# Strided attention on one core: semaphores of the kernel's own, and Q blocks cast whole

## The chip, the core and the metric

The kernel runs on one core of a Trainium2 chip. A core has TensorE (matrix multiply into PSUM), VectorE, ScalarE and GpSimd (elementwise work; the profile calls them PE, DVE, ACT and POOL), SyncE (SP), which here issues all transfers, and 16 DMA rings that carry them. The metric is device time in microseconds, the median of several runs. The profile is of one execution.

## What is computed

Attention in which every query attends to the same 16 keys, those at positions 0, 64, 128 and so on:

```python
batch, heads, seq, dim = (8, 12, 1024, 64)          # stride 64
attend_positions = np.arange(0, seq, stride)        # 16 positions
scores = np.einsum('bhqd,bhkd->bhqk', q, k) * scale # scale = 1/sqrt(dim)
weights = np.exp(scores - np.max(scores, axis=-1, keepdims=True))
weights = weights / (np.sum(weights, axis=-1, keepdims=True) + 1e-10)
result[:, :, i, :] = np.einsum('bhqk,bhkd->bhqd', weights, v)[:, :, 0, :]
```

All of Q (25.2 MB, float32) is read, and a result of the same size is written. Of K and V only 16 rows a head are needed, 0.4 MB each.

## The kernel before

The 96 heads are worked in 24 blocks of 4 heads. A block of Q is 1 MB: a tile `qn` of 128 partitions by 2048 float32. There are 10 `qn` buffers and 8 output buffers `out_sb`, also 1 MB each; `qb`, `qt` and `rec` have 2 each, the weights `w` and the values `v` 3 each.

Setup (lines 88 to 153): SyncE issues K, Q block 0, V and Q blocks 1 to 9. Meanwhile GpSimd builds an identity and the permutation `perm_v` from it (eight small copies, line 118), VectorE and GpSimd clear `k_t`, and VectorE works out which quarter of a group a partition belongs to (lines 132 to 148: `slot_i`, `slot_f`, `s_sel`, `mask`). `key_rows` and `keys` (lines 156 to 175) cast K, transpose it and place it into `k_t`, a third of the heads at a time. `value_rows` (line 177) spreads V over the partitions by a matmul.

A block g goes through these steps:

- `cast(g)`, line 197: float32 to bfloat16. GpSimd takes the first 1024 columns (line 200), ScalarE the other 1024 (line 201).
- `transpose(g)`, line 205: VectorE transposes `qb` into `qt`.
- `scores(g)`, lines 207 to 227: four matmuls (line 212) into one PSUM tile, then two exps on ScalarE (line 223) into `w`.
- `values(g)`, line 189: GpSimd multiplies V with the mask into `v` (line 191). The last 4 columns of `v` give the sum of the weights.
- `outputs(g, c)` for c = 0, 1, 2, line 230: three, two and three matmuls (line 237) into one of two PSUM tiles `o_ps`, then VectorE's reciprocal of the sums (line 245). For c = 0 and 1 VectorE multiplies into `out_sb` (line 247). For c = 2 ScalarE copies (line 249) and GpSimd multiplies in place (line 250).
- `store(g)`, line 252: SyncE issues the output of 1 MB, and then the load of block g+10 (line 298).

The order is written by hand (`ahead`, line 274, and the loop at line 284): in turn g come transpose(g+2), scores(g+1), values(g+2), cast(g+3), then outputs(g, 0..2), store(g) and load(g+10). Every engine works its own instructions in this order. The third of K that is needed later is prepared in turns 1 to 3 and 5 to 7.

The framework puts in the waits: it counts each engine's work with one semaphore an engine, and the transfers with eight, used in turn. So a transfer waits until the eighth before it has landed, and a wait for one instruction can be met only with a later one of the same engine.

Of the kernel before, what the change touches and what calls it, by code (L numbers as in the profile page):

```python
# [11 lines left out]
FP32 = mybir.dt.float32  # L12
BF16 = mybir.dt.bfloat16
# [29 lines left out]

@with_exitstack  # L50
def kernel(
# [24 lines left out]
    const = ctx.enter_context(tc.tile_pool(name="const", bufs=1))  # L76
    qn_pool = ctx.enter_context(tc.tile_pool(name="qn", bufs=QBUFS))
    out_pool = ctx.enter_context(tc.tile_pool(name="outsb", bufs=OBUFS))
    qb_pool = ctx.enter_context(tc.tile_pool(name="qb", bufs=2))
    qt_pool = ctx.enter_context(tc.tile_pool(name="qt", bufs=2))  # L80
    rec_pool = ctx.enter_context(tc.tile_pool(name="rec", bufs=2))
    psum_sc = ctx.enter_context(tc.tile_pool(name="psc", bufs=2, space=bass.MemoryType.PSUM))
    psum_o = ctx.enter_context(tc.tile_pool(name="po", bufs=2, space=bass.MemoryType.PSUM))

    ctx.enter_context(tc.manual_schedule())


    k_raw = const.tile([P, NC, D], FP32, name="k_raw")
    v_raw = const.tile([P, NC, D], FP32, name="v_raw")
    kv_src = [[stride * D, P], [2 * HG * SD, NC], [1, D]]  # L90
    qn = {}

    def load(g):
        qn[g] = qn_pool.tile([P, 32 * D], FP32, name="qn", tag="qn")
        n = P if g < 2 else 32
        _copy(nc, qn[g], _ap_with(Q, [[HG * SD // n, n], [1, HG * SD // n]], g * HG * SD))

    nc.sync.dma_start(k_raw, _ap_with(K, kv_src))
    load(0)
    nc.sync.dma_start(v_raw, _ap_with(V, kv_src))  # L100
# [3 lines left out]

    identity = const.tile([P, P], BF16, name="identity")
    make_identity(nc, identity)
    id_v = identity.rearrange("p (c b a k) -> p c b a k", c=2, b=2, a=2)

    perm_v = const.tile([P, 2, 2, 2, 2, NK], BF16, name="perm_v")

    iota_p = const.tile([P, 1], I16, name="iota_p")
    nc.gpsimd.iota(iota_p, pattern=[[0, 1]], base=0, channel_multiplier=1)
    col4 = const.tile([P, 4], I16, name="col4")
    nc.gpsimd.iota(col4, pattern=[[1, 4]], base=0, channel_multiplier=0)
    for c in range(2):
        for a in range(2):
            for e in range(2):
                nc.gpsimd.tensor_copy(
                    out=perm_v[:, c, a, :, e], in_=id_v[:, c, :, a]
                )  # L120

    k_t = const.tile([P, NG, 2, KW], BF16, name="k_t")
    nc.vector.memset(k_t[:, 0:8], 0.0)  # L123
    w_bufs = []
    for i in range(3):
        w = const.tile([P, 8, P], BF16, name=f"w{i}")
        nc.vector.memset(w, 0.0)  # L127
        w_bufs.append(w)
    nc.gpsimd.memset(k_t[:, 8:NG], 0.0)  # L129
# [9 lines left out]
    nc.vector.tensor_scalar(  # L139
        out=s_sel, in0=col4, scalar1=slot_f, scalar2=None, op0=ALU.is_equal  # L140
    )
    v_bufs = []
    for i in range(3):
        v = const.tile([P, 4 * D + 4], BF16, name=f"v{i}")
        nc.vector.tensor_copy(out=v[:, 4 * D :], in_=s_sel)
        v_bufs.append(v)
    mask = const.tile([P, 4, D], BF16, name="mask")
    nc.vector.tensor_copy(out=mask, in_=s_sel.unsqueeze(2).to_broadcast([P, 4, D]))

    k_bf = const.tile([P, NC, D], BF16, name="k_bf")  # L150
    k_r = const.tile([P, NC, D], BF16, name="k_r")
    v_bf = const.tile([P, NC, D], BF16, name="v_bf")
    v_rep = const.tile([P, NC, 2, D], BF16, name="v_rep")


    def key_rows(m):
        part = slice(4 * m, 4 * m + 4)
        nc.scalar.copy(k_bf[:, part], k_raw[:, part])  # L158
        nc.vector.transpose(  # L159
            k_r[:, part].rearrange("p n d -> p (n d)").bitcast(I32),  # L160
            k_bf[:, part].rearrange("p n d -> p (n d)").bitcast(I32),
        )


    def keys(m, c):
        for s in range(4):
            src, dst, col = 32 * (2 * c + s % 2), 32 * (2 * (s % 2) + s // 2), NK + 32 * s
            op = nc.vector.tensor_copy if m == 0 and s >= 2 else nc.scalar.copy
            op(  # L169
                k_t[dst : dst + 32, 8 * m + c : 8 * m + 8 : 2, :, col : col + NK],  # L170
                k_r[src : src + 32, 4 * m : 4 * m + 4].rearrange(
                    "p n (a k f) -> p a n f k", a=2, f=2
                )[:, s // 2],
            )


    def value_rows(n):
        for c in range(2):
            vp = psum_sc.tile([P, NC // 2, D], FP32, name="vp", tag="sc")
            nc.tensor.matmul(  # L180
                vp, lhsT=perm_v[:, c].rearrange("p a b e k -> p (a b e k)"),
                rhs=v_bf[:, 6 * n : 6 * n + 6], start=True, stop=True,
            )
            nc.vector.tensor_copy(out=v_rep[:, 6 * n : 6 * n + 6, c], in_=vp)  # L184

    qb, qt, wt, vb, rec, out_sb = {}, {}, {}, {}, {}, {}


    def values(g):
        vb[g] = v_bufs[g % 3]  # L190
        nc.gpsimd.tensor_tensor(  # L191
            out=vb[g][:, 0 : 4 * D].rearrange("p (s d) -> p s d", s=4), in0=mask,
            in1=v_rep[:, g // 2, g % 2].unsqueeze(1).to_broadcast([P, 4, D]),
            op=ALU.mult,
        )

    def cast(g):
        qb[g] = qb_pool.tile([P, 32 * D], BF16, name="qb", tag="qb")
        half = 16 * D
        nc.gpsimd.tensor_copy(out=qb[g][:, 0:half], in_=qn[g][:, 0:half])  # L200
        nc.scalar.copy(qb[g][:, half:], qn[g][:, half:])  # L201

    def transpose(g):
        qt[g] = qt_pool.tile([P, 32 * D], BF16, name="qt", tag="qt")
        nc.vector.transpose(qt[g].bitcast(I32), qb[g].bitcast(I32))  # L205

    def scores(g):
        sc = psum_sc.tile([P, 512], FP32, name="sc", tag="sc")
        q = qt[g]
        for e in range(2):  # L210
            for f in range(2):
                nc.tensor.matmul(  # L212
                    sc, lhsT=k_t[:, g, f, NK * (1 - e) : NK * (1 - e) + P],
                    rhs=_ap_with(
                        q, [q.ap[0], [D, 8], [16 * D, 2], [2, 32]],
                        extra_offset=8 * D * e + f,
                    ),
                    start=e + f == 0, stop=e + f == 2,
                )
        w = wt[g] = w_bufs[g % 3]  # L220
        for a in range(2):
            wa = w[64 * a : 64 * a + 64]
            nc.scalar.activation(  # L223
                out=_ap_with(wa, [wa.ap[0], [P, 8], [1, 2], [2, 32]], extra_offset=64 * a),
                in_=sc[64 * a : 64 * a + 64].rearrange("p (t x q) -> p t x q", t=8, x=2),
                func=AF.Exp, bias=0.0, scale=scale,
            )


    def outputs(g, c):  # L230
        if c == 0:
            out_sb[g] = out_pool.tile([P, 4, 8, D], FP32, name="out_sb", tag="out_sb")
            rec[g] = rec_pool.tile([P, 8, 4], FP32, name="rec", tag="rec")
        i0, n = ((0, 3), (3, 2), (5, 3))[c]
        ps = psum_o.tile([P, 3, 512], FP32, name="o_ps", tag="o")
        for i in range(n):
            nc.tensor.matmul(  # L237
                ps[:, i, 0 : 4 * D + 4], lhsT=wt[g][:, i0 + i], rhs=vb[g],
                start=True, stop=True,
            )  # L240
        r = rec[g][:, i0 : i0 + n]
        o = ps[:, 0:n, 0 : 4 * D].rearrange("p i (s d) -> p i s d", s=4)
        to = out_sb[g][:, :, i0 : i0 + n].rearrange("p s i d -> p i s d")
        by = r.unsqueeze(3).to_broadcast([P, n, 4, D])
        nc.vector.reciprocal(r, ps[:, 0:n, 4 * D : 4 * D + 4])  # L245
        if c < 2:
            nc.vector.tensor_tensor(out=to, in0=o, in1=by, op=ALU.mult)  # L247
        else:
            nc.scalar.copy(to, o)  # L249
            nc.gpsimd.tensor_tensor(out=to, in0=to, in1=by, op=ALU.mult)  # L250

    def store(g):
        o = out_sb[g]
        _copy(
# [3 lines left out]
        )  # L258
# [8 lines left out]
    nc.vector.tensor_copy(out=v_bf, in_=v_raw)  # L267
# [16 lines left out]
    for g in range(NG):  # L284
# [13 lines left out]
        if g + QBUFS < NG:  # L298
            load(g + QBUFS)
# [33 lines left out]
```

## Time and profile before

| | |
|---|---|
| median of 3 runs | 129.51 us (129.45 to 129.59) |
| span of the profiled execution, first to last instruction | 127.7 us |
| VectorE busy | 88.5 us (69%), 167 instructions |
| ScalarE busy | 86.1 us (67%), 120 instructions |
| GpSimd busy | 80.1 us (63%), 89 instructions |
| TensorE matmul busy | 63.5 us (50%), 292 instructions |
| moved by the DMA rings | 51.20 MB, 401 GB/s over the span |
| one Q block, from issue to landing | 16.0 us (median) |
| one output, from issue to landing | 14.8 us (median) |

"Busy" is the share of the span in which an engine executes. The time of the runs is taken around the whole program, so it is larger than the span of the profiled execution. The rows for groups of instructions read: line, engine, operation, output <- input, shape, count, busy time in us, mean ns of one, and after the second bar the idle time just before them and what ended most of it. The row of 40 digits for DMA gives the mean busy share of the 16 rings in 40 equal slices of the span, in tenths.

### The profile page before, as it was taken

To read this page: it belongs to the slowest core of one execution; us is meant where nothing else is said; L and a number is where in the kernel's file an instruction comes from. 1 tells how busy PE (TensorE), PEld (TensorE's weight loads), DVE (VectorE), ACT (ScalarE), POOL (GpSimd) and SP (SyncE) were. 2 spreads that over 40 slices of the span, in tenths; PEclk is the share of its full clock that TensorE was granted. 3 is DMA by queue.
4 is the path that set the end of the run, shared out by engine and by line. 5 is a ranking of instruction groups with operands and counts; after the bars stand their busy time and mean duration, and the time that the engine had idled before them with its cause. 6 is when DMAs were issued, how large, how long until landed. Compare 5 with 4: busy or idle time off the path is not lost.

```text
span 127.7 us, 1234 instructions
## 1 busy us (share of the span) xinstructions
PE 63.5 (50%) x292; PEld 29.8 (23%) x292; DVE 88.5 (69%) x167; ACT 86.1 (67%) x120; POOL 80.1 (63%) x89
## 2 busy tenths in 40 slices
PE   0006559256756628653696646366777646410000
PEld 0002223123322313332243313133423313200000
DVE  6956691869698696859769799797987976720000
ACT  4161917886999968999958979979787885320000
POOL 8933709554875876577866997969689694450000
PEclk9999999996799986999559999999856999955555
DMA  2999989998997998989989999999999999999980
GB/s 66 379 320 467 472 349 482 380 452 354 467 482 326 498 413 369 495 362 421 493 357 431 470 380 444 434 403 462 428 393 449 398 428 418 428 426 421 431 352 36
DMA packets 7911, 51.20 MB, mean 401 GB/s; under 512 B 3872, under 2 KB 3872, under 8 KB 3872
## 3 DMA queue, kind: packets, MB, share of 16 engines
q1 hardware_dynamic: 7904, 51.12, 96.7%
q8 instruction: 2, 0.03, 0.1%
q14 instruction: 5, 0.04, 0.1%
HBM read 25.95 MB, written 25.17 MB: 400 GB/s over the span
## 4 chain that ended last, share of the span: by engine, by line
POOL 37%; issue 33%; DVE 10%; PE 6%; ACT 2%; POOLq 1%; DVEq 0%
POOL qb L200 15%; POOL out_sb L250 12%; POOL v L191 10%; PE sc L212 4%; DVE out_sb L247 3%; PE o_ps L237 2%; DVE s_sel L139 2%; POOLq L328 1%; DVE w L127 1%; DVE qt L205 1%; ACT qb L201 1%; DVE rec L245 1%; DVE k_t L123 1%; ACT out_sb L249 1%; ACT k_t L169 0%
## 5 line engine op out<-in xcount | busy, mean ns | idle before, releaser
L237 PE MATMUL o_ps<-v,w 128*128 128x260 bf16 x192 | 37.9, 316 | 37.3 <-DVE out_sb L247 33.2
L250 POOL TENSOR_TENSOR out_sb<-out_sb,rec 128x768 f32<-128x768 f32 x24 | 35.3, 1472 | 29.2 <-ACT out_sb L249 29.2
L247 DVE TENSOR_TENSOR out_sb<-o_ps,rec 128x768 f32<-128x768 f32 (+1 forms) x48 | 39.6, 825 | 1.6
L223 ACT ACTIVATE w<-sc 64x512 bf16<-64x512 f32 x48 | 35.3, 736 | 5.0 <-PE sc L212 4.6
L205 DVE STREAM_TRANSPOSE qt<-qb 128x1024 int32<-128x1024 int32 x24 | 29.5, 1230 | 11.1 <-ACT qb L201 7.1
L212 PE MATMUL sc<-qt,k_t 128*128 128x512 bf16 x96 | 31.7, 463 | 10.4 <-DVE qt L205 10.4
L237 PEld LDWEIGHTS <-w 128*128 128x128 bf16 x192 | 18.6, 108 | 60.5 <-DVE out_sb L247 41.6
L249 ACT COPY out_sb<-o_ps 128x768 f32<-128x768 f32 x24 | 19.2, 800 | 15.8 <-DVE rec L245 15.5
L200 POOL CAST qb<-qn 128x1024 bf16<-128x1024 f32 x24 | 25.0, 1040 | 4.1 <-DMA qn<-in_Q_dram 4.1
L201 ACT CAST qb<-qn 128x1024 bf16<-128x1024 f32 x24 | 25.0, 1047 | 0.7
L245 DVE RECIPROCAL rec<-o_ps 128x12 f32<-128x12 f32 (+1 forms) x72 | 15.1, 210 | 5.6 <-PE o_ps L237 5.2
L191 POOL TENSOR_TENSOR v<-mask,v_rep 128x256 bf16<-128x256 bf16 x24 | 16.1, 670 | 1.0 <-DVE v_rep L184 1.0
L212 PEld LDWEIGHTS <-k_t 128*128 128x128 bf16 x96 | 10.7, 111 | 21.1 <-ACT k_t L169 8.0
L169 ACT COPY k_t<-k_r 32x128 bf16<-32x128 bf16 x20 | 5.9, 296 | 2.3 <-DVE k_r L159 2.0
L129 POOL MEMSET k_t<- 128x4608 bf16 x1 | 3.9, 3937 | 0.0
L184 DVE CAST v_rep<-vp 128x384 bf16<-128x384 f32 x4 | 2.2, 542 | 1.9 <-PE vp L180 1.8
L158 ACT CAST k_bf<-k_raw 128x256 bf16<-128x256 f32 x3 | 1.2, 408 | 2.9 <-DMA k_raw<-in_K_dram 2.9
L139 DVE TENSOR_SCALAR s_sel<-col,slot_f 128x4 bf16<-128x4 int16 x1 | 2.6, 2553 | 0.1
L159 DVE STREAM_TRANSPOSE k_r<-k_bf 128x128 int32<-128x128 int32 x3 | 0.9, 309 | 2.3 <-ACT k_bf L158 2.3
L180 PE MATMUL vp<-v_bf,perm_v 128*128 128x384 bf16 x4 | 1.6, 412 | 1.1 <-DVE v_rep L184 0.6
L158 ACT ACT_TABLE_LOAD x1 | 1.3, 1283 | 0.7 <-PEq L314 0.7
L123 DVE MEMSET k_t<- 128x1152 uint32 x1 | 1.0, 1018 | 1.0 <-PEq L314 1.0
(17 smaller groups left out, 6.6 us busy)
## 6 DMA issues: line engine op xcount, KB each, us to landing
qn<-in_Q_dram SPq DMA_DIRECT2D x24, 1024.0 KB, 16.0
out_dram<-out_sb SPq DMA_DIRECT2D x24, 1024.0 KB, 14.8
k_raw<-in_K_dram SPq DMA_DIRECT2D x1, 384.0 KB, 4.2
v_raw<-in_V_dram SPq DMA_DIRECT2D x1, 384.0 KB, 7.2
```

Source lines behind the costliest of these rows:

```text
L169: op(k_t[dst : dst + 32, 8 * m + c : 8 * m + 8 : 2, :, col : col + NK], k_r[src : src + 32, 4 * m : 4 * m + 4].rearrange("p n (a k f) -> p ...
L191: nc.gpsimd.tensor_tensor(out=vb[g][:, 0 : 4 * D].rearrange("p (s d) -> p s d", s=4), in0=mask, in1=v_rep[:, g // 2, g % 2].unsqueeze(1).t ...
L200: nc.gpsimd.tensor_copy(out=qb[g][:, 0:half], in_=qn[g][:, 0:half])
L201: nc.scalar.copy(qb[g][:, half:], qn[g][:, half:])
L205: nc.vector.transpose(qt[g].bitcast(I32), qb[g].bitcast(I32))
L212: nc.tensor.matmul(sc, lhsT=k_t[:, g, f, NK * (1 - e) : NK * (1 - e) + P], rhs=_ap_with(q, [q.ap[0], [D, 8], [16 * D, 2], [2, 32]], extra_ ...
L223: nc.scalar.activation(out=_ap_with(wa, [wa.ap[0], [P, 8], [1, 2], [2, 32]], extra_offset=64 * a), in_=sc[64 * a : 64 * a + 64].rearrange( ...
L237: nc.tensor.matmul(ps[:, i, 0 : 4 * D + 4], lhsT=wt[g][:, i0 + i], rhs=vb[g], start=True, stop=True,)
L245: nc.vector.reciprocal(r, ps[:, 0:n, 4 * D : 4 * D + 4])
L247: nc.vector.tensor_tensor(out=to, in0=o, in1=by, op=ALU.mult)
L249: nc.scalar.copy(to, o)
L250: nc.gpsimd.tensor_tensor(out=to, in0=to, in1=by, op=ALU.mult)
```

## The change

The framework's tiles, pools and waits go. A small class records every instruction with the names that it reads and writes, works out which waits are needed, and puts them in itself:

```diff
+class Program:
+    ENGINES = ("PE", "DVE", "ACT", "POOL", "SP")
...
+    def op(self, engine, fn, reads=(), writes=(), after=(), lane=None):
+        i = len(self.ops)
+        deps, own = set(after), set()
+        for k in reads:
+            deps.add(self.writer.get(k))
+            own.add(self.writer.get(k))
+        for k in writes:
+            deps.update(self.readers.get(k, ()))
+            deps.add(self.writer.get(k))
+            own.add(self.writer.get(k))
...
+    def plan(self):
...
+            for d in sorted(o["deps"], reverse=True):
+                p = self.ops[d]
+                if p["lane"] == e and (e == "PE" or d not in o["own"]):
+                    continue
+                if known[e].get(p["lane"], -1) >= d:
+                    continue
+                waits.append(d)
+                for k, v in p["done"].items():
+                    known[e][k] = max(known[e].get(k, -1), v)
...
+    def emit(self):
...
+        sems = {lane: self.tc.alloc_semaphore(f"at_{lane}") for lane in counts}
+        with self.tc.tile_critical(no_gpsimd_drain=True):
+            for o in self.ops:
+                for d in o["waits"]:
+                    p = self.ops[d]
+                    engines[o["engine"]].wait_ge(sems[p["lane"]], p["count"])
+                r = o["fn"]()
+                if o["step"]:
+                    r.then_inc(sems[o["lane"]], o["step"])
+            for lane, n in counts.items():
+                if lane.startswith("out"):
+                    nc.sync.wait_ge(sems[lane], n)
```

A wait that follows from an earlier one is left out. An engine counts its semaphore up only at instructions that someone waits for. Each `qn` and each `out_sb` buffer has a transfer semaphore of its own. All instructions stand in one block of the program (`tile_critical`), which every engine enters by a branch after a signal from SyncE, and leaves by another after SyncE has waited for the eight output semaphores.

The cast, from block 4 on, takes a whole block on one engine, even blocks on ScalarE and odd ones on GpSimd:

```diff
     def cast(g):
-        qb[g] = qb_pool.tile([P, 32 * D], BF16, name="qb", tag="qb")
-        half = 16 * D
-        nc.gpsimd.tensor_copy(out=qb[g][:, 0:half], in_=qn[g][:, 0:half])
-        nc.scalar.copy(qb[g][:, half:], qn[g][:, half:])
+        q, b = qn[g % QBUFS], qb[g % 2]
+        if g >= 4:
+            e, fn = ("POOL", nc.gpsimd.tensor_copy) if g % 2 else ("ACT", nc.scalar.copy)
+            op(e, lambda: fn(b, q), reads=[f"qn{g % QBUFS}"], writes=[f"qb{g % 2}0", f"qb{g % 2}1"])
+            return
+        op("POOL", lambda: nc.gpsimd.tensor_copy(out=b[:, 0:half], in_=q[:, 0:half]),
+           reads=[f"qn{g % QBUFS}"], writes=[f"qb{g % 2}0"])
+        op("ACT", lambda: nc.scalar.copy(b[:, half:], q[:, half:]),
+           reads=[f"qn{g % QBUFS}"], writes=[f"qb{g % 2}1"])
```

The wait for a free output buffer is put once, on the value product (which stands in turn g-2), and no longer on the three writers of `out_sb`:

```diff
     def values(g):
-        vb[g] = v_bufs[g % 3]
-        nc.gpsimd.tensor_tensor(
+        v = v_bufs[g % 3]
+        op("POOL", lambda: nc.gpsimd.tensor_tensor(
...
+           after=[stored[g - OBUFS]] if g >= OBUFS else [])
```

In the setup, `perm_v` is made by four copies and not eight, the three `w` buffers are cleared by one memset, the four last columns of the three `v` buffers by one copy, and `s_sel` by two operations on 4 columns:

```diff
-    slot_i = const.tile([P, 1], I16, name="slot_i")
-    nc.vector.tensor_scalar(
-        out=slot_i, in0=iota_p, scalar1=4, scalar2=3,
-        op0=ALU.logical_shift_right, op1=ALU.bitwise_and,
-    )
-    slot_f = const.tile([P, 1], FP32, name="slot_f")
-    nc.vector.tensor_copy(out=slot_f, in_=slot_i)
-    s_sel = const.tile([P, 4], BF16, name="s_sel")
-    nc.vector.tensor_scalar(
-        out=s_sel, in0=col4, scalar1=slot_f, scalar2=None, op0=ALU.is_equal
-    )
+    op("DVE", lambda: nc.vector.tensor_single_scalar(
+        out=slot4, in_=ahead4, scalar=48, op=ALU.bitwise_and
+    ), reads=["ahead4"], writes=["slot4"])
+    op("DVE", lambda: nc.vector.tensor_single_scalar(
+        out=s_sel, in_=slot4, scalar=0, op=ALU.is_equal
+    ), reads=["slot4"], writes=["s_sel"])
```

The order of the steps, the sizes of all transfers and the matmuls are as before.

More of the change, by code (lines that the diff above doesn't have):

```diff
@@ L7 @@
 from concourse import bass_utils, mybir
-from concourse.masks import make_identity
 from concourse._compat import with_exitstack
@@ L142 @@
[L142 to L153, printed above, removed]
+            op("POOL", lambda c=c, a=a: nc.gpsimd.tensor_copy(
+                out=perm_v[:, c, a],
+                in_=id_v[:, c, :, a].unsqueeze(2).to_broadcast([P, 2, 2, NK]),
+            ), reads=["identity"], writes=[f"perm{c}{a}"])
@@ L156, in key_rows @@
+    op("DVE", lambda: nc.vector.tensor_single_scalar(
+        out=s_sel, in_=slot4, scalar=0, op=ALU.is_equal
+    ), reads=["slot4"], writes=["s_sel"])
+    op("DVE", lambda: nc.vector.tensor_copy(
+        out=v_all[:, :, 4 * D :], in_=s_sel.unsqueeze(1).to_broadcast([P, 3, 4])
+    ), reads=["s_sel"], writes=["vs"])
+    op("DVE", lambda: nc.vector.tensor_copy(
+        out=mask, in_=s_sel.unsqueeze(2).to_broadcast([P, 4, D])
+    ), reads=["s_sel"], writes=["mask"])
     def key_rows(m):
         part = slice(4 * m, 4 * m + 4)
-        nc.scalar.copy(k_bf[:, part], k_raw[:, part])
@@ L159, in key_rows @@
-        nc.vector.transpose(
+        op("ACT", lambda: nc.scalar.copy(k_bf[:, part], k_raw[:, part]),
+           reads=["k_raw"], writes=[f"k_bf{m}"])
+        op("DVE", lambda: nc.vector.transpose(
             k_r[:, part].rearrange("p n d -> p (n d)").bitcast(I32),
             k_bf[:, part].rearrange("p n d -> p (n d)").bitcast(I32),
-        )
+        ), reads=[f"k_bf{m}"], writes=[f"k_r{m}"])
     def keys(m, c):
@@ L167, in keys @@
             src, dst, col = 32 * (2 * c + s % 2), 32 * (2 * (s % 2) + s // 2), NK + 32 * s
[L168 to L169 removed]
+            e, fn = ("DVE", nc.vector.tensor_copy) if m == 0 and s >= 2 else ("ACT", nc.scalar.copy)
+            op(e, lambda fn=fn, s=s, src=src, dst=dst, col=col: fn(
                 k_t[dst : dst + 32, 8 * m + c : 8 * m + 8 : 2, :, col : col + NK],
@@ L181, in value_rows @@
                 vp, lhsT=perm_v[:, c].rearrange("p a b e k -> p (a b e k)"),
                 rhs=v_bf[:, 6 * n : 6 * n + 6], start=True, stop=True,
-            )
-            nc.vector.tensor_copy(out=v_rep[:, 6 * n : 6 * n + 6, c], in_=vp)
-    qb, qt, wt, vb, rec, out_sb = {}, {}, {}, {}, {}, {}
+            ), reads=["v_bf"] + [f"perm{c}{a}" for a in range(2)],
+               writes=[f"sc{b}0", f"sc{b}1"])
+            op("DVE", lambda vp=vp, c=c: nc.vector.tensor_copy(
+                out=v_rep[:, 6 * n : 6 * n + 6, c], in_=vp
+            ), reads=[f"sc{b}0", f"sc{b}1"], writes=[f"v_rep{n}{c}"])
@@ L236, in outputs @@
+        o_buf, o_key, to_key = o_ps[t], f"o{t}", f"out{g % OBUFS}{c}"
+        w, v, slot = w_bufs[g % 3], v_bufs[g % 3], out_sb[g % OBUFS]
         for i in range(n):
[L237 to L243, printed above, removed]
+            op("PE", lambda i=i: nc.tensor.matmul(
+                o_buf[:, i, 0 : 4 * D + 4], lhsT=w[:, i0 + i], rhs=v, start=True, stop=True,
+            ), reads=[f"w{g % 3}0", f"w{g % 3}1", f"v{g % 3}", "vs"], writes=[o_key])
@@ L257, in store @@
             _ap_with(o, [o.ap[0], [1, 1], [1, 32 * D]]),
-        )
+        ), reads=[f"out{g % OBUFS}{c}" for c in range(3)], lane=f"out{g % OBUFS}")
     key_rows(0)
@@ L266 @@
     cast(1)
-    nc.vector.tensor_copy(out=v_bf, in_=v_raw)
+    op("DVE", lambda: nc.vector.tensor_copy(out=v_bf, in_=v_raw), reads=["v_raw"], writes=["v_bf"])
     value_rows(0)
```

186 lines of the change are left out of this document (125 added, 61 removed).

## The prediction

> **What bounds the kernel now.** I read the slices and the DMA part of the page first, then the DMA share by microsecond at the end, then what SyncE waits for and when it issues, and only then the engines.
>
> ```profile
> span 127.7 us, 1234 instructions
> ...
> DMA  2999989998997998989989999999999999999980
> GB/s 66 379 320 467 472 349 482 380 452 354 467 482 326 498 413 369 495 362 421 493 357 431 470 380 444 434 403 462 428 393 449 398 428 418 428 426 421 431 352 36
> ...
> q1 hardware_dynamic: 7904, 51.12, 96.7%
> q8 instruction: 2, 0.03, 0.1%
> q14 instruction: 5, 0.04, 0.1%
> ```
>
> The 16 DMA rings are full from about 4 us to about 122 us, reads or writes alike. Q and the output alone are 50.3 MB, and neither version moves a byte less. So the end is set by when the transfers start, by how evenly the 16 rings finish, and by what follows the last landing. The two "instruction" rows matter for the second of these. The end of the transfers, in windows of 1 us (last two columns: DMA share, GB/s):
>
> ```profile
> 122.00:123.00 1.00, 0.00 (x0) 0.00 (x0) 0.00 (x0) 0.00 (x0) 0.00 (x0) 0.50 0.95 401
> 123.00:124.00 1.00, 0.00 (x0) 0.00 (x0) 0.00 (x0) 0.00 (x0) 0.00 (x0) 0.50 0.86 360
> 124.00:125.00 1.00, 0.00 (x0) 0.00 (x0) 0.00 (x0) 0.00 (x0) 0.00 (x0) 0.50 0.31 131
> 125.00:126.00 1.00, 0.00 (x0) 0.00 (x0) 0.00 (x0) 0.00 (x0) 0.00 (x0) 0.50 0.12 49
> 126.00:127.00 1.00, 0.00 (x0) 0.00 (x0) 0.00 (x0) 0.00 (x0) 0.00 (x0) 0.50 0.02 8
> ```
>
> Most rings are done by 124 us; one or two work on until 126.4. The last 2.4 us of the transfers are unevenness. The landing records tell where it comes from. Each transfer lands in 16 parts, one a ring. The latest part is 0.5 us behind the median until 38.6 us. One of the five 8 KB instruction fetches (q14) starts at 39.5 us, and the next transfer has a part 1.3 us behind. One 32 KB packet at 44.2 us takes 1.89 us and not 1.22, and the lag is 2.0, settling at 1.7 us. A fetch at 106.6 us makes it 2.46 us, and it stays so to the end (2.43 us). The 16 KB fetches (q8), at 47.0 and 89.3 us, each put another ring some 1.3 us behind. A fetch thus takes its ring from the data: 0.7 to 0.8 us for 8 KB, about 1.4 us for 16 KB.
>
> ```profile
> SPq L35 <- POOL v L191: 44.3, 11, 7.3
> SPq L35 <- POOL out_sb L250: 23.0, 10, 3.7
> SPq L328 <- DMA out_dram<-out_sb: 11.2, 2, 9.8
> SPq L35 <- DMA qn<-in_Q_dram: 10.8, 6, 2.0
> ...
> SPq L35 <- DMA out_dram<-out_sb: 9.0, 6, 1.9
> ```
> ```profile
> 20.91 0.63 SPq L35 DMA_DIRECT2D out_dram<-out_sb  x1
> ...
> 28.36 0.59 SPq L35 DMA_DIRECT2D out_dram<-out_sb  x1
> ...
> 84.45 31.09 SPq L35 DMA_DIRECT2D out_dram<-out_sb  x10
> ```
>
> These are SyncE's waits (us in total, times, longest) and its issues (start, us). The waits for the compute engines look costly, but the queue never runs dry. Before the second store, at 28.4 us, SyncE has issued 13.4 MB (K, V, eleven Q blocks, one store) and the windows to 28 us have moved 10.3 MB: 3.1 MB, or 7 us, is waiting. At 84.5 us it is 40.6 MB against 34.7: 14 us. The last store is issued at 115.0 us and SyncE then waits 9.8 us for it; its own transfer takes 2.5 us at the 426 GB/s of the windows, so issued by 121.9 us it would land no later.
>
> **The change, part by part.**
>
> *Waits and semaphores.* Transfers no longer wait for the eighth before (10.8 + 9.0 us of SyncE's waits). DVE's reciprocal of the first third no longer waits for the second third's matmuls (at 53.9 us it starts the moment they end). TensorE's weight loads wait together with their matmul. All of this moves compute and issue inside the 7 to 14 us of queued transfers, so I cost it at 0. Without that cover it would be worth up to those waits.
>
> *The casts.* Rows:
>
> ```profile
> L200 POOL CAST qb<-qn 128x1024 bf16<-128x1024 f32 x24 | 25.0, 1040 | 4.1 <-DMA qn<-in_Q_dram 4.1
> L201 ACT CAST qb<-qn 128x1024 bf16<-128x1024 f32 x24 | 25.0, 1047 | 0.7
> ...
> L158 ACT CAST k_bf<-k_raw 128x256 bf16<-128x256 f32 x3 | 1.2, 408 | 2.9 <-DMA k_raw<-in_K_dram 2.9
> ```
>
> 256 columns take ScalarE 0.408 us and 1024 take 1.047, so 2048 take 1.047 + 1024 x 0.00083 = 1.90 us. GpSimd's lie between 1.92 (twice 1.04, less the 0.16 of its smallest copy as the fixed part) and 2.08; I take 1.95. The work per two blocks is as before, but a transpose now waits for one long cast, not two short ones side by side. The longest path this makes goes from the end of one block's first multiply through three blocks: output matmuls 0.51, four score matmuls 1.06, two exps 1.48, ScalarE's cast 1.90, its copy 0.80, GpSimd's multiply 1.47, value product 0.62 (start to start), GpSimd's cast 1.95, transpose 1.25, reciprocal and multiply 1.16: 12.2 us, and with ten handoffs of about 0.04 us 12.6, so 4.2 us a block at worst. Before, stores 2 to 24 come 3.94 us apart ((115.0 - 28.4)/22). At 4.2 the last is issued at 28.4 + 22 x 4.2 = 120.8 us, still before 121.9. Cost 0.
>
> *GpSimd's new wait.* The value product of block g waits until store g-8 has landed; behind it on GpSimd stand the cast and the multiply of block g-2, and SyncE's store behind that. In the trace of before store 16 landed at 106.5 us and the last value product began at 105.0, so late in the run this wait is real, about 1.5 us. Five stores (5 x 2.46 us) are then queued, and multiply plus product need 2.1 us. Cost 0.
>
> *Setup.* Fewer masks and copies ahead of the first transpose (the 2.55 us comparison L139 becomes two on 4 columns, each between 0.10 and 2.55). It moves the first store by at most that; 0.
>
> *Entry and exit.* The streams now stand in a block of their own: one more handshake between SyncE and the others before the first transfer, one more after the last landing, and two more branches an engine. Before, barrier to first transfer takes SyncE 0.06 us, a satisfied wait 0.03, the whole closing barrier 0.17 (127.01 to 127.18), one instruction at the exit about 0.05. Entry: signal, wait, branch, +0.12 (0.05 to 0.2). Exit: branch, signal, drain, five others answer, three waits, branch, wait: seven steps of 0.05, +0.36 (0.2 to 0.7). Both lie on the path, nothing hides them: +0.48.
>
> *Instruction fetches.* Fewer instructions mean fewer fetches. The instruction lists shrink: VectorE 216 to 188, ScalarE 167 to 121, GpSimd 144 to 93, SyncE 101 to 71; TensorE keeps 292 matmuls and 292 weight loads. By the trace VectorE had started 63 instructions at the fetch of 39.5 us and 196 at 106.6. If these two are its own (133 apart, and both hit the latest ring), the second won't come: the new list ends its work at 181. SyncE had started 81 at the fetch of 99.0 us and now has 71. So three 8 KB fetches are left of five. The last ring then stays at 1.72 us if the slow packet of 44.2 us comes again, or at 1.35 (the ring of a 16 KB fetch) if not: 0.71 to 1.08 us earlier; I take 0.9. Bounds for the unknown: 0 (the fetches fall elsewhere, on a ring already late) to 1.9 (only the first 0.5 us is left).
>
> The Trainium skill (Runtime: NRT & Kernel Launch, Instruction fetch mechanics) has refills of 16 KiB, 256 instructions; by it VectorE would have had one fetch at most in this kernel and nothing would be saved (the sum would be 130.0). The trace has 8 KB pieces on q14, five of them, which bears out smaller blocks for all but TensorE.
>
> **Sum.** The profiled execution: span 127.7 us, and 1.8 around it to the median of 129.51. 129.51 + 0.12 + 0.36 - 0.9 = 129.1 us. Its own range, the ends taken crosswise: 129.51 + 0.25 - 1.08 = 128.7 to 129.51 + 0.9 - 0.71 = 129.7.
>
> **The rivals.**
> 1. *The handshakes without the gain: slower.* The fetches that are left, or TensorE's 16 KB, hit a ring that is already 0.5 us late, and the last ring stays 2.4 us behind. For it: the lags come from which ring a fetch hits, and the rings of the two 16 KB fetches differ. Against it: two fetches fewer. It decides once the gain is under 0.48 us. Time 129.51 + 0.48 = 130.0.
> 2. *Evenness all the way: faster.* No ring is hit twice and the slow packet stays out: 129.51 + 0.48 - 1.9 = 128.1. Against it: TensorE's two fetches remain, 1.3 us each.
> 3. *Compute becomes the bound.* The path of alternating casts needs over 4.25 us a block ((121.9 - 28.4)/22), say 4.4: last store at 125.2, 3.3 late, 133.3 us. For it: VectorE already waits 7.1 us in all for ScalarE's casts. Against it: 4.2 is my worst case.
> 4. *A branch into the new block has to fetch its target.* Nothing is hidden at entry or exit; one 16 KB fetch took 1.05 us, so 129.1 + 1.1 = 130.2 at least. Against it: the branch before the first transfer fits in 0.06 us, with no fetch near it. The same section of the skill says that a taken branch whose target is outside the current two pages stalls for a fetch; the trace has two branches an engine and none did.
>
> That the change doesn't do what it says I leave out: the built lists show its own waits alone.
>
> **How the numbers follow.** Forecast 48%, rival 1 25%, rival 2 12%, rival 3 6%, rival 4 9%. 0.2% (0.26 us) is what this kernel's measurement tells from no change. Four fifths of the forecast I put below 129.25, as both ends must be bad at once to get above it: faster 0.39 + 0.12 = 0.51. Same: 0.09 of the forecast and 0.08 of rival 1, which spreads by its exit cost over 129.7 to 130.3: 0.17. Slower: the rest of rival 1 and rivals 3 and 4: 0.32. The range reaches from 128.2, which takes in most of rival 2, to 130.4 (rivals 1 and part of 4).
>
> **What would show it.** Right: q14 with three fetches, the lag of the last part under 1.8 us, the DMA slices as full as now, the last landing to the end of the span 1.2 to 1.3 us (now 0.9), first transfer at about 0.86 us (now 0.74). Wrong: slices with a DMA share below 0.9 in mid run (compute starves the queue), a last store issued after 121.9, or a lag that is again 2.4 us.

## The result: slower, because the queue of transfers ran dry at the end

| | before | changed |
|---|---|---|
| median | 129.49 us (129.24 to 129.92, 20 runs) | 130.62 us (129.51 to 131.89, 20 runs) |
| span of the profiled execution | 127.7 us | 129.1 us (its own time 130.94 us) |
| last store issued | 115.0 us | 123.4 us |
| last landing | 126.83 us | 127.62 us |
| last landing to end of span | 0.89 us | 1.51 us |
| first packet | 1.83 us | 2.06 us |

The ratio of the changed kernel to the one before is 1.0069, with an interval of 1.0045 to 1.0093. The runs of the changed kernel spread over 2.4 us, those of the kernel before over 0.7. Ratios here and below leave out runs over 1.5% above the fastest of their kernel or at a lower clock, which are four of the changed kernel's 20; the median of its other 16 is 130.49 us.

From the page of the changed kernel, the span, the row of DMA shares and the instruction fetches:

```profile
span 129.1 us, 1076 instructions
...
DMA  1999999998998998999999999989989999998493
...
q14 instruction: 3, 0.02, 0.0%
```

The bytes are the same and the 8 KB instruction fetches (q14) have gone from five to three, as forecast. What is new is the end of the DMA row: 8, 4, 9, 3, where the kernel before had 9, 9, 8, 0. Windows of 4 us of the changed kernel show it closer (each window: its length, then the busy time of TensorE, its weight loads, VectorE, ScalarE and GpSimd; last three columns: granted TensorE clock, DMA share, GB/s):

```profile
108.00:112.00 4.00, 3.62 (x12) 1.62 (x12) 2.63 (x6) 2.21 (x3) 4.00 (x4) 0.50 1.01 426
112.00:116.00 4.00, 3.27 (x12) 1.61 (x12) 1.76 (x5) 1.56 (x3) 1.60 (x2) 0.51 1.01 424
116.00:120.00 4.00, 1.72 (x11) 0.64 (x10) 3.40 (x9) 1.57 (x3) 1.15 (x2) 0.92 0.88 365
120.00:124.00 4.00, 0.73 (x3) 0.17 (x2) 0.91 (x2) 0.80 (x1) 2.00 (x2) 0.50 0.63 258
124.00:128.00 4.00, 0.00 (x0) 0.00 (x0) 0.00 (x0) 0.00 (x0) 0.00 (x0) 0.50 0.68 281
```

Up to 116 us the rings are full. Then they wait for the compute engines, which still work at 123 us; in the kernel before these had ended by 115. The prediction had named this as a sign of being wrong: a last store issued after 121.9 us. SyncE's issues of the stores in the changed kernel (the second, the ninth, and the ten from the fifteenth on), and its wait for the outputs:

```profile
28.67 0.59 SPq L34 DMA_DIRECT2D out_dram<-out_sb  x1
...
61.16 0.59 SPq L34 DMA_DIRECT2D out_dram<-out_sb  x1
...
87.12 36.82 SPq L34 DMA_DIRECT2D out_dram<-out_sb  x10
```
```profile
SPq L124 <- DMA out_dram<-out_sb: 3.5, 2, 2.8
```

The last store is issued at 87.12 + 36.82 - 0.59 = 123.35 us. SyncE then waits for the outputs 2.8 us at the longest; before, the last store had been queued so early that this wait was 9.8. From the last issue to the last landing is 4.27 us, so the store issued at 123.35 lands at 127.6. The pace of the stores, in us a block (the last column is `e1_split` of the experiments, the changed kernel with halves):

| stores | before | changed | changed, with halves |
|---|---|---|---|
| 2 to 9 | 4.47 | 4.64 | 4.53 |
| 9 to 15 | 4.13 | 4.33 | 3.87 |
| 15 to 24 | 3.39 | 4.03 | 3.97 |
| 2 to 24 | 3.94 | 4.30 | 4.12 |

Against the kernel before, the last stretch has changed most. Against halves it is the middle one, but the last stretch of halves is held up by something else: their stores come early enough to use up the free output buffers, and GpSimd's value product waits 2.9 us for one.

```profile
POOL v_all L277 <- DMA out_dram<-out_sb: 2.9, 2, 1.6
```

The rows of the casts, and of the transposes that wait for them, in the changed kernel:

```profile
L298 DVE STREAM_TRANSPOSE qt<-qb 128x1024 int32<-128x1024 int32 x24 | 29.6, 1232 | 16.3 <-POOL qb L290 8.4
...
L290 ACT CAST qb<-qn 128x2048 bf16<-128x2048 f32 x10 | 19.0, 1898 | 0.2
L290 POOL CAST qb<-qn 128x2048 bf16<-128x2048 f32 x10 | 18.9, 1892 | 0.0
```

The durations are those of the prediction (1.90; GpSimd's 1.89 and not 1.95). But the transposes now wait longer for casts, before first and changed second:

```profile
DVE qt L205 <- ACT qb L201: 7.1, 7, 3.0
DVE qt L205 <- POOL qb L200: 4.1, 6, 0.8
```
```profile
DVE qt L298 <- POOL qb L290: 8.4, 9, 1.6
DVE qt L298 <- ACT qb L290: 3.3, 3, 1.9
DVE qt L298 <- ACT qb L294: 3.0, 1, 3.0
DVE qt L298 <- POOL qb L292: 1.5, 1, 1.5
```

That is 11.2 us in all before and 16.2 now (L292 and L294 are the halves of the first four blocks). The chain of waits of the changed kernel, two blocks of it in order of time (start, us, what), shows why:

```profile
85.70 1.25 DVE qt L298
...
88.20 0.69 DVE out_sb L341
88.89 0.15 DVE rec L338
89.06 0.81 ACT out_sb L344
...
89.94 1.47 POOL out_sb L345
91.41 0.63 POOL v_all L277
92.04 1.84 POOL qb L290
...
93.91 1.25 DVE qt L298
```

This is a closed loop. The transpose stands ahead of the block's multiplies on VectorE, the multiplies lead to ScalarE's copy, the copy to GpSimd's multiply, and behind that, in program order, stand the value product and the long cast that the transpose two turns later needs. Once round takes 93.91 - 85.70 = 8.21 us, 4.1 a block, and no engine is busy all the way: it is a latency. With halves, GpSimd's part of that loop is some 0.85 us shorter (1.89 less 1.04), and the kernel before did 3.39 a block in the last stretch.

This is not the path that the prediction added up: ScalarE's cast, the exps and the matmuls aren't on it. That longer path is in the trace too, from 66.6 us on, in a stretch in which TensorE's clock was granted at little over half (0.53 over 60 to 76 us):

```profile
66.65 0.83 PE o L330 x3
67.48 1.72 PE sc L306 x4
...
70.73 1.90 ACT qb L290
...
75.62 1.84 POOL qb L290
...
77.49 1.25 DVE qt L298
...
78.89 0.96 DVE out_sb L341
```

From the end of one block's first multiply (66.60) to that of the third block after it (79.85) are 13.25 us, 4.4 a block. The matmuls are 2.55 us of it, where the prediction had 0.51 + 1.06.

In an earlier stretch the chain goes through ScalarE instead. Here it copies K into `k_t` between its other work (changed kernel, chain of waits):

```profile
34.59 1.90 ACT qb L290
...
36.51 0.80 ACT out_sb L344
...
37.34 0.30 ACT k_t L251
...
38.56 0.74 ACT w_all L317
39.31 0.74 ACT w_all L317
```

From the second store to the ninth ScalarE is busy 28.0 of 31.3 us before and 27.1 of 32.5 now; 4.7 us of either are copies into `k_t`.

Late in the run TensorE's clock differs as well. The windows of 104 to 116 us show how it was granted, before first and changed second; whether the casts have to do with that, these runs don't tell:

```profile
104.00:116.00 12.00, 4.18 (x23) 1.92 (x23) 6.87 (x16) 4.62 (x7) 6.07 (x5) 0.83 1.01 425
```
```profile
104.00:116.00 12.00, 9.48 (x36) 4.48 (x36) 8.15 (x17) 6.66 (x9) 7.39 (x7) 0.57 1.01 425
```

At 0.50 four score matmuls take 1.71 us and not 1.06. The clock alone doesn't sort the runs, though: over its span the profile of halves has 0.795 and full rings to the end, that of `e3_wait_moved` 0.832 and a dry queue.

### The profile page after: what moved, and what is told of

Read it like the earlier page. It is cut to its first block, busy times and chain, and to the rows that moved or that the text cites. A ratio compares the mean times of both kernels' runs of the same rounds, so it can differ in the third digit from the quotient of the medians.

```text
span 129.1 us, 1076 instructions
## 1 busy us (share of the span) xinstructions
PE 68.3 (53%) x292; PEld 30.6 (24%) x292; DVE 89.0 (69%) x162; ACT 84.7 (66%) x110; POOL 78.0 (60%) x74
## 4 chain that ended last, share of the span: by engine, by line
DVE 27%; ACT 25%; POOL 23%; PE 12%; DMA 5%; issue 3%; SPq 0%; DVEq 0%
DVE out_sb L341 12%; DVE qt L298 10%; POOL out_sb L345 9%; POOL qb L290 9%; ACT out_sb L344 8%; ACT w_all L317 7%; PE sc L306 6%; PE o L330 6%; ACT qb L290 6%; DMA qn<-in_Q_dram 5%; DVE rec L338 4%; POOL v_all L277 3%; ACT k_t L251 3%; POOL qb L292 2%; ACT qb L294 1%
## 5 line engine op out<-in xcount | busy, mean ns | idle before, releaser
L330 PE MATMUL o<-v_all,w_all 128*128 128x260 bf16 x192 | 40.3, 337 | 40.0 <-DVE out_sb L341 35.4
L341 DVE TENSOR_TENSOR out_sb<-o,rec 128x768 f32<-128x768 f32 (+1 forms) x48 | 39.6, 824 | 1.6
L317 ACT ACTIVATE w_all<-sc 64x512 bf16<-64x512 f32 x48 | 35.3, 735 | 8.0 <-PE sc L306 7.5
L330 PEld LDWEIGHTS o<-v_all,w_all 128*128 128x128 bf16 x192 | 19.0, 115 | 64.3 <-DVE out_sb L341 44.5
L344 ACT COPY out_sb<-o 128x768 f32<-128x768 f32 x24 | 19.2, 799 | 22.8 <-DVE rec L338 22.5
L290 ACT CAST qb<-qn 128x2048 bf16<-128x2048 f32 x10 | 19.0, 1898 | 0.2
L290 POOL CAST qb<-qn 128x2048 bf16<-128x2048 f32 x10 | 18.9, 1892 | 0.0
L277 POOL TENSOR_TENSOR v_all<-mask,v_rep 128x256 bf16<-128x256 bf16 x24 | 16.1, 669 | 1.2 <-DVE v_rep L271 1.1
L306 PEld LDWEIGHTS sc<-qt,k_t 128*128 128x128 bf16 x96 | 11.2, 118 | 22.2 <-DVE qt L298 11.3
L292 POOL CAST qb<-qn 128x1024 bf16<-128x1024 f32 x4 | 4.2, 1038 | 4.9 <-DMA qn<-in_Q_dram 4.9
L294 ACT CAST qb<-qn 128x1024 bf16<-128x1024 f32 x4 | 4.1, 1044 | 0.2 <-DMA qn<-in_Q_dram 0.2
## 6 DMA issues: line engine op xcount, KB each, us to landing
out_dram<-out_sb SPq DMA_DIRECT2D x24, 1024.0 KB, 12.6
```

The source lines that it names most:

```text
L277: op("POOL", lambda: nc.gpsimd.tensor_tensor(out=v[:, 0 : 4 * D].rearrange("p (s d) -> p s d", s=4), in0=mask, in1=v_rep[:, g // 2, g % 2] ...
L290: op(e, lambda: fn(b, q), reads=[f"qn{g % QBUFS}"], writes=[f"qb{g % 2}0", f"qb{g % 2}1"])
L292: op("POOL", lambda: nc.gpsimd.tensor_copy(out=b[:, 0:half], in_=q[:, 0:half]), reads=[f"qn{g % QBUFS}"], writes=[f"qb{g % 2}0"])
L306: op("PE", lambda e=e, f=f: nc.tensor.matmul(sc, lhsT=k_t[:, g, f, NK * (1 - e) : NK * (1 - e) + P], rhs=_ap_with(q, [q.ap[0], [D, 8], [16 ...
L317: op("ACT", lambda a=a, wa=wa: nc.scalar.activation(out=_ap_with(wa, [wa.ap[0], [P, 8], [1, 2], [2, 32]], extra_offset=64 * a), in_=sc[64 ...
L330: op("PE", lambda i=i: nc.tensor.matmul(o_buf[:, i, 0 : 4 * D + 4], lhsT=w[:, i0 + i], rhs=v, start=True, stop=True,), reads=[f"w{g % 3}0" ...
```

## Experiments

The theory after the result: whole casts lengthen the loop, so the stores come late (A). The rivals: the own semaphores cost the time, by the handshakes of their block or by GpSimd's new wait for a free output buffer.

### All casts in halves, and whole casts alone

`e1_split` is the changed kernel without its branch for whole casts:

```diff
-        if g >= 4:
-            e, fn = ("POOL", nc.gpsimd.tensor_copy) if g % 2 else ("ACT", nc.scalar.copy)
-            op(e, lambda: fn(b, q), ...)
-            return
```

> The changed kernel with every Q block cast in two halves again (the semaphores of its own stay). Theory A, the alternating whole casts make compute too slow to feed the rings: the last store is issued at 113 to 118 us and not 123.4, the rings stay full to about 123 us, 129.0 to 129.6 us, and the runs spread by less than 0.6 us. Theory B, the new waits slow compute (weight loads that wait with their matmul, the out-buffer wait on GpSimd): the last store stays after 122 us and the time at 130 to 131 us.

`e2_whole_only` is the kernel before, with its framework's waits, and whole casts:

```diff
     def cast(g):
...
+        if g >= 4:
+            (nc.gpsimd.tensor_copy if g % 2 else nc.scalar.copy)(qb[g], qn[g])
+            return
```

> The kernel before with the whole casts alone, even blocks from 4 on by ScalarE and odd ones by GpSimd; the framework's semaphores stay. Theory A: the last store is issued at 121 to 125 us, 129.8 to 131.5 us with a spread of 1 us and more, as in the changed kernel. Theory B: within 0.3 us of the kernel before, last store at about 115.

Halves: 129.71 us (129.41 to 130.17), ratio 1.0019 (1.0007 to 1.0031). Whole casts alone: 130.59 us (129.73 to 131.56), ratio 1.0085 (1.0057 to 1.0114). The DMA row of the whole casts alone, and SyncE's last issues:

```profile
DMA  2999989998998998998998999989989999995885
```
```profile
87.88 36.33 SPq L35 DMA_DIRECT2D out_dram<-out_sb  x10
```

With halves:

```profile
DMA  1999999898998998989989989999999999999970
```
```profile
83.43 36.29 SPq L34 DMA_DIRECT2D out_dram<-out_sb  x10
```

With whole casts alone the last slices are as empty as in the changed kernel and the last store comes at 123.62, while with halves the rings stay full and it comes at 119.1. So the casts make the loss, whoever puts in the waits. What is left for the semaphores, with all else that the change has, is 0.25 us. Halves missed each bound of their expectation by a little: the last store (119.1 and not 113 to 118), the time (129.71 and not 129.0 to 129.6) and the spread (0.76 us and not under 0.6).

### The wait for a free output buffer

`e3_wait_moved` is the changed kernel with that wait back on the writers of `out_sb`:

```diff
-        ), reads=["mask", f"v_rep{g // 12}{g % 2}"], writes=[f"v{g % 3}"],
-           after=[stored[g - OBUFS]] if g >= OBUFS else [])
+        ), reads=["mask", f"v_rep{g // 12}{g % 2}"], writes=[f"v{g % 3}"])
...
+        free = [stored[g - OBUFS]] if g >= OBUFS else []
...
-                reads=[o_key, r_key], writes=[to_key])
+                reads=[o_key, r_key], writes=[to_key], after=free)
...
```

> The changed kernel with the wait for a free output buffer back on the three writers of out_sb. Theory A: nothing changes, 130 to 131 us, since no value product is seen to wait for a store in the trace of the changed kernel. Theory B in the form that this wait holds up GpSimd: 129.5 us, last store before 120.

131.57 us (129.87 to 131.64), ratio 1.0125 (1.0082 to 1.0168): over both expectations. Nothing is gained, and the last store comes at 124.1. The interval overlaps the changed kernel's, so a loss by this edit is not shown either. In the changed kernel's trace no value product is seen to wait for a store. With halves two are, 2.9 us in all, but the rings are full all the same.

### Whole casts, but a turn earlier

`e4_cast_early` keeps the work of the whole casts and takes them out of the loop: `cast(g + 4)` in turn g, not `cast(g + 3)`, and three `qb` buffers.

```diff
-    qb = [sb.tile([P, 32 * D], BF16, name=f"qb{i}") for i in range(2)]
+    qb = [sb.tile([P, 32 * D], BF16, name=f"qb{i}") for i in range(3)]
...
+    cast(3)
...
-        if g + 3 < NG:
-            cast(g + 3)
+        if g + 4 < NG:
+            cast(g + 4)
```

> The changed kernel with whole casts, each issued one turn earlier (cast(g+4) in turn g, three qb buffers). The engines' work is the same. Theory A in the form that the latency of the loop transpose, ScalarE copy, GpSimd multiply, value product, GpSimd cast sets the pace (8.2 us for two blocks): the transposes no longer wait for GpSimd's cast, the last store comes before 119 us, 129.0 to 129.7 us. Theory A in the form that the engines' load sets it: 130 to 131 us as before.

130.12 us (129.77 to 130.22), ratio 1.0046 (1.0030 to 1.0062). The DMA row, SyncE's last issues and VectorE's waits for casts:

```profile
DMA  1999999897998999989989989999999999999970
```
```profile
81.79 35.88 SPq L34 DMA_DIRECT2D out_dram<-out_sb  x10
```
```profile
DVE qt L298 <- ACT qb L294: 1.2, 1, 1.2
```

The rings are full to the end again, the last store comes at 117.1, and the only wait for a cast left is for one of the first four. The same casts, a turn earlier and with the third buffer that this takes, don't bind: it was the latency. But the time stayed above what was expected (129.0 to 129.7), 0.4 us over halves. Two later runs come back to this.

### Whole casts in one part of the run only

`e8_whole_first_ten` and `e9_whole_last_ten` are the changed kernel with one line changed:

```diff
-        if g >= 4:
+        if 4 <= g < 14:
```
```diff
-        if g >= 4:
+        if g >= 14:
```

> The changed kernel with whole casts for blocks 4 to 13 alone, halves from block 14 on. Theory A (the loss is that the last stores come too late: the loop with whole casts takes 4.0 to 4.6 us a block in every stretch, and only the last stretch has no time left to catch up): the first part comes 2 to 3 us late, the halves catch up at 3.4 to 3.9 us a block, the last store is issued by 120 us and the time is that of halves throughout, 129.5 to 130.0. Rival B (the loss is made in the first part, where ScalarE still copies K and the exps queue behind its whole cast, and isn't recovered): 130.3 to 130.9.

> The changed kernel with halves up to block 13 and whole casts for blocks 14 to 23 alone. Theory A: block 14's store at about 85 us as before, then nine steps of 4.0 to 4.1 us: last store at 121 to 122, just at the 121.9 from which it decides: 129.7 to 130.3, and nearer the upper end where TensorE's clock is low. Rival B (the loss is made in the first part): 129.5 to 129.8 and a last store before 118.

SyncE's last ten stores, whole casts in blocks 4 to 13 first, in 14 to 23 second:

```profile
86.42 32.49 SPq L34 DMA_DIRECT2D out_dram<-out_sb  x10
```
```profile
84.49 36.84 SPq L34 DMA_DIRECT2D out_dram<-out_sb  x10
```

With whole casts first the fifteenth store is late (86.4, with halves 83.4), but nine steps of 3.54 us bring the last to 118.3, and the time is 129.79 us (129.50 to 129.99), that of halves. So halves that come late do catch up. With whole casts last, nine steps of 4.03 us lead to 120.7 (121 to 122 was expected), and the rings stay full:

```profile
DMA  1999899997989989989999989989989899999990
```

The time is 130.05 us (129.90 to 130.68), 0.34 over halves, but not because of the stores: the spans are those of halves (127.7 to 128.5 us, halves 127.6 to 128.4), and the difference lies outside the span, where these runs spend 2.2 us and halves 1.8. So neither part of the whole casts costs anything within the span. Delay is made in both, and only together do they run the queue dry.

### What the own semaphores cost

`e5_second_block` doubles the handshake of the block, on top of halves:

```diff
+        with self.tc.tile_critical(no_gpsimd_drain=True):
+            nc.sync.wait_ge(sems["k_raw"], 16)
+            nc.sync.nop()
```

> The changed kernel with every cast split in halves (129.71 us, 0.25 over before), and behind the waits for the outputs a second block of the program that holds one satisfied wait and nothing else: one more entry and one more exit handshake on the path, no other work. Theory A (the block costs 0.23 us at its entry and 0.6 at its exit, and that is what eats the gain of the fetches): +0.7 to +0.9 us, 130.4 to 130.6; last landing to the end of the span about 2.2 us, not 1.5. Rival B (the handshake hides behind something at the program's end, and what the split version lacks is the gain itself): within 0.2 us of 129.71, and last landing to the end of the span 1.5 to 1.7.

130.43 us (130.11 to 130.94), ratio 1.0086 (1.0066 to 1.0107). That is 0.7 us over halves, and last landing to end of span is 2.28 us and not 1.50. The handshake is on the path.

`e7_no_block` takes it away: halves, own waits, and the streams stand in the program's first block. With the block go the framework's closing barriers; GpSimd, and not SyncE, waits for the outputs.

```diff
-        with self.tc.tile_critical(no_gpsimd_drain=True):
-            for o in self.ops:
...
-                    nc.sync.wait_ge(sems[lane], n)
+        for o in self.ops:
...
+                nc.gpsimd.wait_ge(sems[lane], n)
+        nc.clear_and_free_semaphores(list(sems.values()))
...
-    with _tile.TileContext(nc) as tc:
-        tile_strided_attention_kernel(tc, *args)
+    tc.nc = nc
+    tile_strided_attention_kernel(tc, *args)
```

> The changed kernel with every cast split in halves (129.71 us), its streams now in the program's first block: no entry or exit by a branch and a signal, and no closing barriers of the framework; GpSimd waits for the eight outputs and clears the semaphores, and the other engines just end. Same instructions otherwise. Theory A (the block's handshakes are what the own semaphores cost): first packet 0.24 us earlier, last landing to the end of the span 0.2 to 0.6 us and not 1.5, the last ring 1.2 to 2.1 us late as before: 128.2 to 129.1, faster than both kernels. Rival B (what lies outside the span grows as the closing barriers go, since the runtime waits for every engine anyway): span shorter but 129.3 to 129.8.

128.68 us (128.48 to 128.95), ratio 0.9948 (0.9930 to 0.9966): faster than both kernels. From its page:

```profile
DMA  2999999997989989999999999989899899999992
...
q14 instruction: 3, 0.02, 0.0%
```

The first packet is at 1.834 us again (with the block 2.056 to 2.069), and last landing to end of span is 0.39 us. Halves in the block have spans of 127.6 to 128.4 us, without it 126.3 to 126.8. Not all of that is gained: the time of the runs is 2.1 us above their span, and with the block that was 1.8. The rival expected this in full; it came to 0.3 us. Whether the missing barriers cause it is not shown, as `e9_whole_last_ten` has the block and its runs are 2.2 us above their span as well. In the profiles of these two kernels and of the next one, an 8 KB instruction fetch starts 1.6 to 2.1 us after the end of the span, in the others none later than 1.2; no run tests whether that has to do with it.

`e8_no_block_cast_early` is the same with whole casts a turn early.

> The same without the block, but with whole casts one turn earlier and three buffers for them (130.12 us with the block). Theory A: down by the same amount as halves: 128.6 to 129.5. Rival B (whole casts one turn early have a cost of their own, some 0.4 us over halves, that isn't the block's): 0.3 to 0.5 us over the halves of this call.

128.73 us (128.44 to 129.08), ratio 0.9950 (0.9932 to 0.9967), the same as halves. `e9_before_cast_early` does that with the waits of the kernel before (whole casts as in `e2_whole_only`, `cast(g + 4)` and three buffers as in `e4_cast_early`).

> The kernel before, its waits and semaphores as they were, with whole casts from block 4 on, one turn earlier and in three buffers. Theory A (the wait on one long cast is the only harm of whole casts, and a turn of lead hides it): rings full to the end, last store issued before 121.9, fetches as before: 129.2 to 129.8. Rival B (whole casts cost something else, by the load they put on two engines in turn): 130.0 to 130.6, as with whole casts in the old place (130.59).

129.35 us (129.12 to 130.84) beside 129.45, ratio 1.0008 (0.9984 to 1.0032), last store at 120.1. So whole casts cost nothing of their own where they are a turn ahead. Why that form was 0.4 us over halves inside the block stays open; 0.2 of it is a longer exit in its profile (1.73 us from the last landing to the end, 1.50 with halves), in which VectorE comes to the closing barrier 0.77 us after the last landing, with halves 0.40.

### What a fetch costs

`e6_more_fetches` is halves, with 30 long-met waits behind each store, so that SyncE's list is 360 instructions longer:

```diff
+                if o["lane"].startswith("out"):
+                    for _ in range(30):
+                        nc.sync.wait_ge(sems["k_raw"], 16)
```

> The changed kernel with every cast split in halves, and behind each store 30 waits on the semaphore of K's load, long met, so that SyncE's list is some 360 instructions longer and nothing moves a byte or waits. Theory A (each 8 KB instruction fetch takes a ring 0.7 to 0.8 us away from the data, and the last ring sets the end): five or six 8 KB fetches in place of three, the last ring later by 0.7 us where a fetch hits the latest ring and by nothing where it hits another: 130.0 to 131.2. Rival B (fetches don't set the end): 129.6 to 129.8.

131.75 us (131.52 to 131.81), ratio 1.0184 (1.0167 to 1.0202), more than expected. From its page:

```profile
DMA  2999989998998999998998998998998999999930
...
q14 instruction: 6, 0.05, 0.1%
```

The stores come as early as with halves (last one at 118.9). But two fetches at 42.9 and 43.4 us, another at 75.6 and one at 108.1 take ring time. By the landing records the last ring is 1.9 us behind the median at 70 us, 2.5 at 80 and 3.7 at 110, after the fetch of 108.1; the last landing is at 128.52 us. So fetches move the end where they fall on a ring that is already late: three more of them, and 2.0 us more than halves. Some 0.4 us of the lag grows between 80 and 105 us, without an 8 KB fetch; where that comes from stays open.

## Why the prediction was wrong, step by step

- **The casts: the step that failed.** "4.2 us a block at worst", last store "at 120.8 us, still before 121.9", "Cost 0", and 6% for compute becoming the bound. The 4.2 was no worst case: stores 2 to 24 came 4.30 us apart, the last at 123.35, and the cost was 0.8 us (130.49 against 129.71 with halves). Two things were left out. The early stretch was slower than 4.2 already, 4.47 before and 4.64 now, with ScalarE busy nine tenths of it before the change, its copies of K included; an average over all stores, 3.94, hides that. And the path was priced at TensorE's full clock: where half was granted, it took 13.25 us and not 12.6, so 4.4 a block. What whole casts then took away is the fast last stretch that caught up (3.54 where halves come late, 4.03 with whole casts). Replacing only its 3.39 by the 4.1 of the loop gives 28.4 + 7 x 4.47 + 6 x 4.13 + 9 x 4.1 = 121.4 us, half a microsecond from the limit, and the 0.2 us a block by which the first two stretches grew as well brings it past. That the late loop's 4.1 lies so near to 4.2 is chance, since it is another path. How much of the loss is the half clock, no run sets apart. Rival 3 named the mechanism; its 4.4 us a block is there only where the clock was half, and its 133.3 us was too large.
- **Where the limit lies.** 121.9 us was nearly right. With the queue dry, the last landing comes 4.25 to 4.27 us after the last issue in three profiles (the changed kernel, `e2_whole_only`, `e3_wait_moved`), so before's 126.83 us is passed from 122.6 on. The step is gentle, since with a dry queue the rings finish evenly (last ring under 0.1 us behind in these three): a store issued 8.4 us later landed 0.8 later.
- **Waits and GpSimd's new wait at 0: borne out**, by `e1_split` and `e3_wait_moved`. The wait that the prediction saw coming is there with halves (2.9 us), and full rings cover it. The packets before had moved 34.3 MB at 84.5 us, not 34.7; that makes 15 us of queue and changes nothing. Setup at 0: nothing in these runs speaks against it; it was not tried alone.
- **Entry and exit: right mechanism, sizes too small.** +0.12 was +0.22 by the first packet; +0.36 was +0.62 by the last landing. `e5_second_block` (about +0.7) and `e7_no_block` (about -1.0, closing barriers included) agree with both, that it is on the path and how long it is.
- **Instruction fetches: right, the gain somewhat too large.** Three were left of five. The last ring was 1.38 us behind in the changed kernel at 118 us, 1.05 less than before, against a forecast of 0.71 to 1.08. It gained nothing there, because the queue ran dry and evened the rings out. In seven other profiles with three such fetches before the last landing and full rings to the end (`e1_split`, `e4_cast_early`, `e5_second_block`, `e8_whole_first_ten`, `e9_whole_last_ten`, and the two without a block) the last ring is 1.23 to 2.13 us behind, and in `e9_before_cast_early`, with five, 2.5 as before. So 0.3 to 1.2 is the gain, with the slow packets below as the scatter. That the two 16 KB fetches (q8) are TensorE's, no run shows.
- **The sum with the casts at 0** would be 129.51 + 0.22 + 0.62 less 0.3 to 1.2, which is 129.15 to 130.05; halves measured 129.71. So even with the casts right, the change was not faster: the handshakes eat the gain of the fetches. That is rival 1's balance, but not its reason, as the last ring did not stay 2.4 us behind. Of the 1.4 us between the forecast 129.1 and 130.49, 0.8 are the casts, 0.36 the handshakes; the rest, some 0.25, would be a gain from the fetches smaller than 0.9.
- **Rival 4 did not come.** In the changed kernel SyncE's branch at the entry takes 0.03 us, and no 8 KB or 16 KB fetch is near the entry or the exit. The "two branches an engine" that the prediction reads off the trace of before are not recorded there under any name.

## What to carry to other kernels

Where a hand-ordered pipeline hides behind full transfers, compute has a budget to the last store, and it must be summed stretch by stretch: a change that slows the fast stretch takes away the catching up, though the average still looks safe. A "worst case" has to hold at the clock that the trace grants, not only at the full one. Two short pieces of work on two engines side by side and one long piece on one engine are the same load but not the same latency; a longer piece needs a turn more of lead and one more buffer. And what one pays once, at the entry and exit of a program, counts in a kernel that is bound by transfers: without the block of their own and its closing barriers, and with halves, the same semaphores make this kernel 0.5% faster than it was.

## What was not expected of the hardware

Some 32 KB packets take 1.3 to 2.3 us where the others take 1.22. One kind starts at the moment at which an 8 KB instruction fetch ends, and takes 1.5 to 1.9 us: in the changed kernel at 43.6 and 68.3 us. This suggests that a fetch of 0.31 us costs its ring more than its own time. The other kind has no fetch beside it. Many of these lie near the same times in different kernels, about 10.1 us apart: in the kernel before at 44.2 and 74.4 us (and 63.8, 73.8), with halves at 54.3 and 64.4 (and 63.8), with early casts at 54.3. Others don't fit that, as the changed kernel's at 78.5 and that of `e9_whole_last_ten` at 58.8. The ring that they hit stays behind to the end, as after a fetch: with halves the last ring goes from 1.2 us behind at 51 us to 2.2 at 71, in two steps, after the packets of 54.3 and 64.4. What they are, no run here shows. They set as much of the unevenness as a fetch does, so the gain of fewer fetches is seen only over several runs.
